# Two of the four sums of weight quadrants in each set of seven products are formed by adding transfers from DRAM instead of by VectorE

## The chip, the core and the metric

The kernel runs on one core of one Trainium2 chip, in one launch. The metric is the device time of that launch in microseconds (us); before the change the median of three runs is 1113.65 us (1112.79 to 1114.22). The core has five engines that run side by side and wait for each other on semaphores: PE (TensorE, matrix products; PEld in the profile is its loading of stationary operands), DVE (VectorE), ACT (ScalarE), POOL (GpSimd) and SP (SyncE, which here only issues transfers). Each engine takes its own instructions strictly in order, so an instruction that waits holds up everything behind it on that engine. Transfers (DMAs) are issued from the queue of an engine, here SP's or POOL's, wait there like any instruction, and run on the core's 16 DMA engines.

## The reference

A model of two layers on 512 tokens of width 1024, all in float32. Each layer mixes tokens (a gated spatial unit in the first layer, forgetting attention in the second, with attention to a memory beside both), then runs a feed-forward network of hidden width 2816. What matters here is the feed-forward network, once per layer:

```python
D_FF = -(-8 * D_MODEL // (3 * 256)) * 256
...
    h = h + rmsnorm(mixed @ w_out[layer], ln_mix_post[layer])
    f = rmsnorm(h, ln_ffn_pre[layer])
    f = (jax.nn.silu(f @ w_ffn_gate[layer]) * (f @ w_ffn_up[layer])) @ w_ffn_down[layer]
    h = h + rmsnorm(f, ln_ffn_post[layer])
```

## The kernel before

**Products in three parts.** Float32 products are made of three products in a rounded format (fp32r). Every operand is split into a high and a low part: ACT casts (`hi`, line 239), DVE subtracts (`lo`, line 240; both in `split`). `mm3` (lines 182 to 184) then issues hi·hi, hi·lo and lo·hi into one PSUM tile. Weights come from DRAM as 128 x 1024 blocks of 512 KB, called `raw`, into a ring of four buffers; `parts` turns 128 x 512 of such a block into a pair of parts, in a ring of eight pairs.

**Sets of seven products.** From the third block of 128 hidden rows on, `feed_forward` takes gate and up weights two blocks at a time. The 256 x 1024 weights of such a pair of blocks and the 1024 x 512 inputs are each cut into four quadrants, and the 2 x 2 product of quadrants is formed with seven products in place of eight, after Strassen and Winograd. That is class `Seven`: one set for gate, one for up, then the next pair of blocks. Ten pairs per layer make 20 sets, in two layers 40. Each product is 12 matmuls of 128 x 256, so a set is 84.

A set loads two blocks (line 1007): the first holds the quadrants a11 and a12 side by side, the second a21 and a22. `sums` forms four sums on DVE: s3 = a11 + a21 (line 1022, in a buffer of its own), a21 + a22 in place of a21 (line 1024), that sum + a11 in place of a11 (line 1026), and that + a12 in place of a12 (line 1027). Between them a11 and a12 are split as they came. `run` issues product by product, and splits what it needs: product 1 uses a11, 2 uses a12, 7 uses s3, 6 the new a11, 4 uses a22, 3 the new a12 and 5 the new a21. The order is 1, 7, 2, 6, 4, 3, 5. The first pair of each layer (`plain_first`) is different: both sets run 1, 2 and 3, then each runs 7 and 6, then each 4 and 5.

**PSUM.** A set has three PSUM tiles, x, a and e, of one tag, `mm` for gate and `lg` for up, with three buffers each: the third set of a layer writes the banks of the first, the fourth those of the second. A set's tiles are drained by ACT copies (lines 1040, 1049, 1052, 1055) and by `end` on DVE: e at line 1060, a at line 1061, x at line 1063. `rows` (lines 1110, 1116 and 1118) turns the results into gated hidden rows.

**Around the sets.** After three or two pairs the hidden rows go through the down weights: six or four 512 KB blocks per group, in the same ring of four raw buffers, with DVE adding the results (line 1174). Before the sets of a layer come the boundary (line 907), which norms the inputs and runs the first two hidden blocks in the ordinary way, and `combined` (line 973), in which DVE forms sums of input quadrants.

**What sets the order.** A tile framework records the program, gives each tile a buffer, places waits, and orders the instructions of each engine by its own estimate of when they can start; each engine then follows that order. So a buffer that comes free earlier may be taken by a later tile, and the order on DVE, ACT, POOL and SP is not that of the source. All weight loads are on SP's queue. POOL does little: it raises small tiles to the power −1/2 for the norms (line 253) and issues four 128 KB transfers (line 382). The s3 tile comes from a ring of four 128 x 512 buffers (`temp`, tag `t`), which a set holds until its product 7 is split.

Of the kernel before, what the change touches and what calls it, by code (L numbers as in the profile page):

```python
# [11 lines left out]
ALU = mybir.AluOpType  # L12
# [30 lines left out]
def hybrid(ctx: ExitStack, tc: tile.TileContext, i: dict, out: bass.AP):  # L43
    nc = tc.nc
# [11 lines left out]
    def name(s):  # L56
        n_of[s] = n_of.get(s, 0) + 1
        return f"{s}_{n_of[s]}"
# [7 lines left out]
    def prob(s, shape=(P, T)):  # L66
        return tp.tile(list(shape), F32, tag="p", name=name(s), bufs=6)

    def temp(s, shape=(P, T), tag="t", bufs=4, dt=F32):
        return tp.tile(list(shape), dt, tag=tag, name=name(s), bufs=bufs)  # L70
# [4 lines left out]
    def ps(tag, shape=(P, T), s="ps"):  # L75
        return pp.tile(list(shape), F32, tag=tag, name=name(s), bufs=2 if tag == "tr" else 3)

    V, A, PE, G = nc.vector, nc.scalar, nc.tensor, nc.gpsimd
# [53 lines left out]
    def loaded(src):  # L132

        raw = wp.tile([P, 1024], F32, tag="raw", name=name("raw"), bufs=4)
        last_load[0] = nc.sync.dma_start(raw, src)
        return raw
# [118 lines left out]
    class Norm:  # L255


        def __init__(self, width=T):
            self.r4 = small("r4")
            self.acc, self.width = None, width  # L260
# [25 lines left out]
        def sums(self, tb, cols):  # L286
            return [self.acc[:, c + tb * P : c + (tb + 1) * P] for c in range(0, T, self.width)]
# [711 lines left out]
    class Seven:  # L999
# [5 lines left out]
        def __init__(self, xs, src, tag, rows):  # L1005
            self.xs, self.rows = xs, rows
            w1, w2 = loaded(src(0)), loaded(src(1))
            self.a = [w[:, d : d + 512] for w in (w1, w2) for d in (0, 512)]
            self.x, self.p = ps(tag, s="x"), ps(tag, (P, 256), s="a")
            self.q = ps(tag, (P, 256), s="e")  # L1010
            self.s1, self.s2 = prob("s1"), prob("s2")
# [6 lines left out]
        def sums(self):  # L1018

            a11, a12, a21, a22 = self.a  # L1020
            self.s3 = temp("s3")
            V.tensor_add(self.s3, a11, a21)
            self.w1 = self.parts(a11)
            V.tensor_add(a21, a21, a22)
            self.w2 = self.parts(a12)
            V.tensor_add(a11, a21, a11)
            V.tensor_add(a12, a11, a12)
# [470 lines left out]
```

## Time and profile before

| What | Value |
|---|---|
| Median of three runs | 1113.65 us (1112.79 to 1114.22) |
| Span of the profiled execution | 1111.4 us |
| Mean granted TensorE clock | 0.998 |
| Instructions in the profile | 19500 |
| Read from HBM, written | 104.71 MB, 2.10 MB |
| Mean transfer rate over the span | 106 GB/s |

The profile is of one execution. Its span runs from the first to the last instruction, and the measured times hold a little around it. A row of a group gives line, engine, operation, what is written and read (out<-in), the shape and a count, then busy time, mean duration of one in ns, and the time for which the engine stood idle just before such instructions, with what ended it. A row of a timeline gives start and duration in us; instructions that follow each other are merged, with their count. `SPq` is an issue of a transfer on SP's queue. The time of a transfer to landing is counted from its issue. Tile names have lost their numbers: every weight buffer is `raw`, and `s` is both s3 and the results of a set.

### The profile page before, as it was taken

What the parts mean: (1) busy time and instruction counts of PE and PEld (TensorE: products, weight loads), DVE (VectorE), ACT (ScalarE), POOL (GpSimd) and SP (SyncE); (2) the same over time, 40 slices, a digit from 0 to 9 for tenths busy, and PEclk for the clock granted to TensorE, in tenths of its full rate; (3) what the DMA queues carried; (4) which work ended last, traced back from release to release, by engine and by line L of the source; (5) the groups of instructions that cost most, each with busy time, mean ns of one, the idle gap of its engine ahead of it and who ended that gap; (6) DMA issues with size and microseconds to landing.
All of it is one profiled execution on the core that took longest, in us unless ns stands there. A gap on an engine that the chain in (4) does not pass through costs nothing.

```text
span 1111.4 us, 19500 instructions
## 1 busy us (share of the span) xinstructions
PE 1100.8 (99%) x7382; PEld 1000.1 (90%) x7382; DVE 893.7 (80%) x1735; ACT 660.5 (59%) x1397; POOL 25.3 (2%) x42
## 2 busy tenths in 40 slices
PE   9999999999999999999999999999999999999997
PEld 7998889998899898998988898889999899899996
DVE  8889658997697597896987898858997697687875
ACT  8776468664365264577665667668665265254553
POOL 0100000000000000001000000000000000000000
PEclk9999999999999999999999999999999999999999
DMA  7522322334133323343322654422224133333222
GB/s 267 162 76 77 98 74 76 115 109 141 57 112 97 117 92 114 97 148 117 104 88 62 173 132 116 131 76 74 79 90 154 62 114 96 101 109 114 77 76 76
DMA packets 64421, 118.12 MB, mean 106 GB/s; under 512 B 5260, under 2 KB 40088, under 8 KB 64328
## 3 DMA queue, kind: packets, MB, share of 16 engines
q1 hardware_dynamic: 63720, 116.18, 33.4%
q8 instruction: 58, 0.95, 0.4%
q0 software_dynamic: 192, 0.52, 0.2%
q14 instruction: 35, 0.29, 0.1%
q10 hardware_dynamic: 416, 0.18, 0.1%
HBM read 104.71 MB, written 2.10 MB: 96 GB/s over the span
## 4 chain that ended last, share of the span: by engine, by line
PE 94%; ACT 3%; DVE 1%; issue 1%; POOL 0%; DMA 0%; POOLq 0%; DVEq 0%; ACTq 0%
PE y L182 10%; PE y L183 10%; PE y L184 10%; PE a L182 5%; PE a L184 5%; PE a L183 5%; PE x L184 3%; PE e L182 3%; PE e L184 3%; PE e L183 3%; PE x L183 3%; PE x L182 3%; PE ps L184 3%; PE ps L183 3%; PE ps L182 3%; PE v L182 2%
## 5 line engine op out<-in xcount | busy, mean ns | idle before, releaser
L239 ACT CAST whi<-raw 128x512 fp32r<-128x512 f32 x460 | 273.1, 620 | 217.7 <-PE y L184 89.1
L240 DVE TENSOR_TENSOR wlo<-raw,whi 128x512 fp32r<-128x512 f32 x460 | 303.5, 684 | 69.5 <-ACT whi L239 67.8
L182 PE MATMUL y<-whi,fhi 128*128 128x512 f32 (+1 forms) x356 | 140.2, 394 | 0.4 <-DVE y L838 0.4
L184 PE MATMUL y<-whi,flo 128*128 128x512 f32 (+1 forms) x356 | 139.3, 391 | 0.0
L183 PE MATMUL y<-wlo,fhi 128*128 128x512 f32 (+1 forms) x356 | 139.2, 391 | 0.0
L184 PE MATMUL x<-xshi,wlo 128*128 128x256 f32 x320 | 89.9, 281 | 0.0
L182 PE MATMUL a<-xshi,whi 128*128 128x256 f32 x320 | 89.8, 281 | 0.0
L183 PE MATMUL x<-xslo,whi 128*128 128x256 f32 x320 | 89.7, 280 | 0.0
L182 PE MATMUL x<-xshi,whi 128*128 128x256 f32 x320 | 89.7, 280 | 0.0
L183 PE MATMUL a<-xslo,whi 128*128 128x256 f32 x320 | 89.7, 280 | 0.0
L184 PE MATMUL a<-xshi,wlo 128*128 128x256 f32 x320 | 89.6, 280 | 0.0
L184 PEld LDWEIGHTS y<-whi,flo 128*128 128x128 f32 x356 | 66.8, 188 | 15.7
L182 PEld LDWEIGHTS y<-whi,fhi 128*128 128x128 f32 x356 | 66.8, 188 | 15.6 <-DVE y L838 0.7
L183 PEld LDWEIGHTS y<-wlo,fhi 128*128 128x128 f32 x356 | 66.9, 188 | 14.7
L182 PEld LDWEIGHTS a<-xshi,whi 128*128 128x128 f32 x320 | 60.2, 188 | 0.5
L183 PEld LDWEIGHTS a<-xslo,whi 128*128 128x128 f32 x320 | 60.2, 188 | 0.3
L184 PEld LDWEIGHTS x<-xshi,wlo 128*128 128x128 f32 x320 | 60.3, 188 | 0.0
L183 PEld LDWEIGHTS x<-xslo,whi 128*128 128x128 f32 x320 | 60.2, 188 | 0.0
L184 PEld LDWEIGHTS a<-xshi,wlo 128*128 128x128 f32 x320 | 60.2, 188 | 0.0
L182 PEld LDWEIGHTS x<-xshi,whi 128*128 128x128 f32 x320 | 60.2, 188 | 0.0
L183 PE MATMUL ps<-xslo,whi 128*128 128x256 f32 x192 | 53.9, 283 | 0.6 <-DVE xslo L240 0.6
L184 PE MATMUL ps<-xshi,wlo 128*128 128x256 f32 x192 | 54.4, 285 | 0.0
(297 smaller groups left out, 3111.1 us busy)
## 6 DMA issues: line engine op xcount, KB each, us to landing
raw<-in_w_gate SPq DMA_DIRECT2D x44, 512.0 KB, 3.5
raw<-in_w_up SPq DMA_DIRECT2D x44, 512.0 KB, 3.6
raw<-in_w_down SPq DMA_DIRECT2D x44, 512.0 KB, 3.8
raw<-in_w_out SPq DMA_DIRECT2D x16, 512.0 KB, 4.8
raw<-in_w_b_q SPq DMA_DIRECT2D x8, 512.0 KB, 3.4
raw<-in_w_a_u SPq DMA_DIRECT2D x6, 512.0 KB
raw<-in_w_v SPq DMA_DIRECT2D x6, 512.0 KB, 4.3
raw<-in_w_k SPq DMA_DIRECT2D x6, 512.0 KB
```

Source lines behind the costliest of these rows:

```text
L182: PE.matmul(o, w[0], x[0], start=start, stop=False, skip_group_check=more)
L183: PE.matmul(o, w[0], x[1], start=False, stop=False, skip_group_check=more)
L184: return PE.matmul(o, w[1], x[0], start=False, stop=stop, skip_group_check=more)
L239: last_hi[0] = A.copy(hi, src)
L240: last_split[0] = last_hi[0], (eng or V).tensor_sub(lo, src, hi)
```

## The change

```diff
--- before.py
+++ after.py
@@ -1006,6 +1006,10 @@
             self.xs, self.rows = xs, rows
             w1, w2 = loaded(src(0)), loaded(src(1))
             self.a = [w[:, d : d + 512] for w in (w1, w2) for d in (0, 512)]
+            self.s3 = temp("s3")
+            nc.sync.dma_start(self.s3, src(0)[:, :512])
+            for dst, d in ((self.s3, 0), (self.a[2], 512)):
+                G.dma_start(dst, src(1)[:, d : d + 512], accum_op=ALU.add)
             self.x, self.p = ps(tag, s="x"), ps(tag, (P, 256), s="a")
             self.q = ps(tag, (P, 256), s="e")
             self.s1, self.s2 = prob("s1"), prob("s2")
@@ -1018,10 +1022,7 @@
         def sums(self):
 
             a11, a12, a21, a22 = self.a
-            self.s3 = temp("s3")
-            V.tensor_add(self.s3, a11, a21)
             self.w1 = self.parts(a11)
-            V.tensor_add(a21, a21, a22)
             self.w2 = self.parts(a12)
             V.tensor_add(a11, a21, a11)
             V.tensor_add(a12, a11, a12)
```

For s3, SP loads a11 once more into the buffer of s3 (256 KB), and POOL issues a transfer of a21 from DRAM that adds to what the buffer holds. For a21 + a22, POOL issues a transfer of a22 from DRAM that adds to a21 where the weight load put it. The two additions on DVE are gone; those that make the new a11 and the new a12 stay. Per set that is one more issue on SP and two on POOL, and 768 KB more from DRAM.

In the order of the changed program, the a11 addition of a set is the first DVE instruction that waits for the sum a21 + a22. On POOL the adding transfer of a21 + a22 for the first set of each layer stands before the boundary's two powers (line 253), and that for the second set after them. On SP the load for s3 of set n + 4 stands before the weight loads of set n + 2. In the third set of each layer DVE has, in this order: the splits of a11 and a12 as they came, the split of s3, the a11 addition, the a12 addition, the split of the new a11, the drain of the first set's e, the splits of a22 and of the new a12, and the drains of the first set's a and x. PE's products of the third set wait for these drains: the first product for e's, the second for a's, the third for x's.

## The prediction

> **What bounds the kernel now.** I read the page first: busy time by engine, then the chain that ended last.
>
> ```profile
> PE 1100.8 (99%) x7382; PEld 1000.1 (90%) x7382; DVE 893.7 (80%) x1735; ACT 660.5 (59%) x1397; POOL 25.3 (2%) x42
> PE 94%; ACT 3%; DVE 1%; issue 1%; POOL 0%; DMA 0%; POOLq 0%; DVEq 0%; ACTq 0%
> ```
>
> PE is busy for 99% of the span, and 94% of the chain is PE. A share over the whole run can hide a stage with another limit, so next come the stretches: columns are time, then busy time of PE, PEld, DVE, ACT and POOL, granted clock, DMA share, GB/s. The first three hold sets of seven products in layer 0, the fourth in layer 1, the last is the kernel's tail.
>
> ```profile
> 203.00:242.00 39.00, 39.00 (x331) 38.94 (x330) 36.70 (x66) 24.50 (x53) 0.00 (x0) 1.00 0.34 109
> 242.00:263.00 21.00, 21.00 (x178) 20.89 (x177) 17.50 (x32) 11.62 (x27) 0.00 (x0) 1.00 0.39 121
> ...
> 296.00:356.00 60.00, 60.00 (x508) 59.87 (x507) 50.61 (x88) 34.94 (x72) 0.00 (x0) 1.00 0.32 105
> 788.00:850.00 62.00, 62.00 (x516) 61.47 (x515) 56.19 (x100) 37.37 (x80) 0.00 (x0) 1.00 0.34 111
> ```
>
> ```profile
> 1077.00:1111.00 34.00, 26.74 (x144) 22.09 (x142) 21.99 (x57) 15.41 (x34) 2.19 (x4) 0.95 0.22 62
> ```
>
> In every stretch with sets PE is busy without a break: 39.00 of 39.00, 60.00 of 60.00. DVE reaches 94% in the first (36.70 of 39.00), yet PE never waits for it there. All idle PE time of the run is 1111.4 − 1100.8 = 10.6 us, and 34.00 − 26.74 = 7.3 of it lies in the tail, which has no sets. So at most 3.3 us elsewhere could be won at all, none of it inside the sets.
>
> **What is removed.** Two additions on DVE per set, 40 sets (columns: count, busy us, mean ns of one, idle before it).
>
> ```profile
> L1024 DVE TENSOR_TENSOR raw<-raw 128x512 f32<-128x512 f32 x40 | 27.4, 684 | 0.2
> L1022 DVE TENSOR_TENSOR s<-raw,raw 128x512 f32<-128x512 f32 x40 | 27.4, 684 | 13.2 <-DMA raw<-in_w_gate 13.2
> ```
>
> That is 54.8 us of DVE work. I value it at nothing: PE's uninterrupted work in the stretches above covers it. If that cover were gone, if PE waited for DVE, it would be worth up to 54.8 us.
>
> **What is added, off the path.** (a) 40 loads of 256 KB on SP's queue. An issue takes 0.33 us (rows below), 13 us in all. They stand among the weight loads; each waits only for the split of the s3 four sets earlier, which stands before the last split of the buffer that the next weight load needs, so on SP they hold up little: the one place where that counts is in the sum. (b) 120 transfers of 256 KB, 31.5 MB more from DRAM.
>
> ```profile
> q1 hardware_dynamic: 63720, 116.18, 33.4%
> ```
>
> At 33.4% of the DMA engines for 116 MB, and counting an adding transfer twice since it must also read what it adds to, 40 × 0.26 + 80 × 0.52 = 52 MB make 15% more: under half busy on average, so nothing. (c) 80 issues on POOL. The nearest rows are four POOL transfers of 128 KB.
>
> ```profile
> L382 POOL DMA_DIRECT2D memk<-memk x4 | 2.3, 572 | 312.2 <-DVE memk L380 312.2
> ```
>
> At 0.57 us for 64 rows I take 1.1 us for 128 rows (bounds 0.57 and, twice my value, 2.3); two of them per set of 9.9 us leave POOL room. But in the changed program's order the adding transfer of the first set of each layer stands on POOL ahead of the reciprocal square root that PE's broadcast waits for.
>
> ```profile
> 172.65 0.34 SPq L135 DMA_DIRECT2D raw<-in_w_gate  x1
> ...
> 179.88 0.99 POOL L253 TENSOR_TENSOR r<-var,mhalf 128x2 f32<-128x2 f32 x1 [12.29 <-ACT sq L308]
> ```
>
> Its weights are issued at 172.65 and land 4.9 us later at most (measured below), 177.5; 1.1 us on POOL ends at 178.6, 1.3 before 179.88, and even 2.3 ends at 179.8. Nothing, then; what an issue takes beyond 2.4 us would come on top, once per layer.
>
> **What is added on the path: the wait for a21 + a22.** s3 is begun four sets ahead and cannot be late unless an adding transfer takes tens of us. The other sum can: load of the second weight tile, landing, wait on POOL, adding transfer, and only then DVE's a11 addition (L1026 before). How much time that has depends on the place. The tightest of the ordinary sets is the fifth of a layer:
>
> ```profile
> 228.80 0.33 SPq L135 DMA_DIRECT2D raw<-in_w_gate  x1
> ```
>
> ```profile
> 246.83 0.28 PE L182 MATMUL a<-d2hi,whi 128*128 128x256 f32 x1
> ```
>
> Issued at 228.80 and landed 4.9 us later, 233.7, its weights are there 13 us before PE's first product with that sum, and the addition with its split takes 2 of these. The exception is the third set of each layer, the first after the pair that runs its plain products first: its load is issued late, and in the changed order DVE has the a11 addition, with its new wait, ahead of the additions that drain the first set's PSUM tiles, whose banks the third set's first products write. Queued behind it are, in this order: the a12 addition, one split, the drain of e (frees the bank for the third set's first product), two splits, the drain of a (frees the bank for the second product). Here is that place before, on SP, DVE and PE (start us, duration us).
>
> ```profile
> 212.46 0.33 SPq L135 DMA_DIRECT2D raw<-in_w_gate  x1
> ```
>
> ```profile
> 798.66 0.33 SPq L135 DMA_DIRECT2D raw<-in_w_gate  x1
> ```
>
> ```profile
> 199.81 0.68 DVE L1022 TENSOR_TENSOR s<-raw,raw 128x512 f32<-128x512 f32 x1
> 200.41 0.68 DVE L240 TENSOR_TENSOR wlo<-raw,whi 128x512 fp32r<-128x512 f32 x1
> ...
> 217.33 0.69 DVE L1022 TENSOR_TENSOR s<-raw,raw 128x512 f32<-128x512 f32 x1 [0.42 <-DMA raw<-in_w_gate]
> ...
> 219.38 0.68 DVE L1026 TENSOR_TENSOR raw<-raw,raw 128x512 f32<-128x512 f32 x1
> 219.98 0.41 DVE L1060 TENSOR_TENSOR s<-e,s 128x256 f32<-128x256 f32 x1
> 220.32 0.68 DVE L1027 TENSOR_TENSOR raw<-raw 128x512 f32<-128x512 f32 x1
> 220.91 0.68 DVE L240 TENSOR_TENSOR wlo<-raw,whi 128x512 fp32r<-128x512 f32 x1
> 221.60 0.43 DVE L1061 TENSOR_TENSOR s<-a,s 128x256 f32<-128x256 f32 x1
> ```
>
> ```profile
> 803.61 0.69 DVE L1022 TENSOR_TENSOR s<-raw,raw 128x512 f32<-128x512 f32 x1 [0.62 <-DMA raw<-in_w_gate]
> ```
>
> ```profile
> 222.79 0.28 PE L182 MATMUL a<-xshi,whi 128*128 128x256 f32 x1
> ...
> 224.21 0.28 PE L182 MATMUL e<-t3hi,whi 128*128 128x256 f32 x1
> ```
>
> ```profile
> 808.92 0.28 PE L182 MATMUL a<-xshi,whi 128*128 128x256 f32 x1
> ...
> 810.33 0.28 PE L182 MATMUL e<-t3hi,whi 128*128 128x256 f32 x1
> ```
>
> Even before, DVE waited here for the landing (0.42 and 0.62 us), and the drains ended at 222.03, 0.8 us before PE's first product.
>
> *Landing.* From issue to the end of DVE's wait: 217.33 − 212.46 = 4.87, and 803.61 − 798.66 = 4.95. Four of the removed additions stand between 199.81 and the split that frees this buffer. DVE starts full 128x512 instructions 0.60 apart (200.41 − 199.81), so the load goes out up to 2.4 us earlier; I take 2.1, since casts on ACT sit between (bounds 0 and 2.4). The new 256 KB load goes ahead of it.
>
> ```profile
> raw<-in_w_gate SPq DMA_DIRECT2D x44, 512.0 KB, 3.5
> ...
> raw<-in_w_mem_k SPq DMA_DIRECT2D x4, 512.0 KB, 7.5
> ...
> memk<-memk POOLq DMA_DIRECT2D x4, 128.0 KB, 2.7
> ...
> out<-h SPq DMA_DIRECT2D x3, 128.0 KB, 1.9
> ```
>
> Between 128 KB in 1.9 us and 512 KB in 3.5 lie 4.2 us per MB, so 256 KB is 1.1 us; half of it overlaps, 0.6. Landing: 212.46 − 2.1 + 4.87 + 0.6 = 215.8 and 798.66 − 2.1 + 4.95 + 0.6 = 802.1.
>
> *Adding transfer.* No row shows one. Lower bound:
>
> ```profile
> DMA to landing us min/median/max: 2.4/2.7/4.8
> ```
>
> 2.4 us, the quickest POOL transfer of half the size; upper bound 7.5, the slowest group of 512 KB loads. I take 5.7: the median POOL transfer 2.7, plus 1.6 for moving 512 KB in place of 128 at 4.2 us per MB (256 KB from DRAM, as much from SBUF), plus 1.4 for the two other weight loads in flight there (4.87 against 3.5). A long tail beyond 7.5 can't be excluded, since neither row adds anything.
>
> The Trainium skill, "DMA: Bandwidth & Descriptors", section "Anatomy of one DMA — SWDGE (gpsimd) path", gives a POOL-issued transfer about 2.0 us plus its bytes at 436 GB/s, an estimate of 2.6 us for 256 KB; the sum would then be nothing. For 128 KB it gives 2.3 against the 2.7 measured here, so it is near, but it is stated for plain transfers and no trace here shows an adding one.
>
> *From there to PE.* After the sum lands at time t, DVE needs 0.60 + 0.60 + 0.75 (a cast first) + 0.35 + 0.60 + 0.60 + 0.42 = 3.9 us to the end of the second drain, and PE's second product wants it at 224.21 and 810.33: t may be 220.3 and 806.4. It is 215.8 + 5.7 = 221.5 and 802.1 + 5.7 = 807.8: late by 1.2 and 1.4 us. PE then runs behind for good, since it has no idle time to catch up in.
>
> **Sum.** Against the profiled execution, 1111.4 + 2.6 = 1114.0. The measured median, 1113.65, is 2.3 us above that span, which no edit touches, so the forecast is **1116.3 us**. The unit of measurement that can be told from no change is 0.2%, 2.2 us; the forecast is only just past it.
>
> **Rivals.**
> *Hidden.* The sum lands within 4.4 us; PE never notices: 1113.7. For it: the 2.7 us POOL transfers and the skill's rule. Against: the transfers in flight at just that place. This ends on the other side, not slower. It decides at 220.3 − 215.8 = 4.5 and 806.4 − 802.1 = 4.3 us.
> *Slow addition.* An adding transfer takes 10 us: 5.5 us at each of the two places, 1124.7, with about 1 us more per layer at the fifth set. Above some 9.6 us the ring of four weight buffers turns into the bound. Two sets take PE 2 × 7 × 1.42 = 19.9 us (12 matmuls from 222.79 to 224.21); load 4.9, transfer, and seven splits and two additions at 0.60, 5.4, have to fit. At 15 us it would cost 2.7 us on each of some 36 sets, about 1210 us. For it: no row shows an adding transfer. Against: POOL rows at 2.4 to 4.8.
> *Relief reaches PE.* DVE's freed 54.8 us shorten the 3.3 us that PE loses outside the tail: if two thirds or more went, 1111.4. Against: those gaps lie outside the sets, with other instructions waited for.
>
> **Chances.** Forecast (4.4 to 9 us per adding transfer, 1113.7 to 1123) 0.48, of which 0.33 past the bound; hidden 0.26; slow 0.21; relief 0.05. Slower by over 0.2%: 0.33 + 0.21 = 0.54. Within: 0.15 + 0.24 + 0.01 = 0.40. Faster: 0.02 + 0.04 = 0.06. Range 1112.5 to 1128: it takes in the hidden case with a us of scatter and the slow one up to about 11 us; what it leaves out is a far slower transfer and half of the relief. The forecast's own range is 1113.7 to 1123.
>
> **What would show it.** Landing of the adding transfers: 4.5 to 7 us, longest where four loads are in flight. POOL: some 1.1 us per issue. DVE busy down by about 55 us, PE busy the same. Around 222 and 809 us PE idle 1 to 1.5 us before the third set's first two products, released by the drains on DVE, and DVE idle ahead of the a11 addition, ended by a POOL transfer. No such PE gap: hidden. PE gaps before later sets too, or a11 additions waiting in most sets: slow addition. A gap before the broadcast near 181 and 767 us would say that POOL's queue was the price. A shorter time with PE's idle unchanged would break the whole argument, since then the pace of the matmuls themselves would have moved.

## The result and the profile after

The changed kernel takes 1122.99 us (median of 4 runs, 1122.20 to 1124.84) against 1113.56 us (4 runs, 1112.79 to 1114.22): ratio 1.0088, 95% interval 1.0073 to 1.0102. It is slower by 9.4 us; the forecast's sum was 2.6. The profiled execution has a span of 1120.7 us, 9.3 above that of before.

The page of the changed kernel: busy time, then two DMA queues (packets, MB, share of 16 engines), then the chain that ended last.

```profile
PE 1104.6 (99%) x7382; PEld 1003.8 (90%) x7382; DVE 850.9 (76%) x1655; ACT 662.1 (59%) x1397; POOL 94.0 (8%) x122
...
q1 hardware_dynamic: 69480, 126.67, 36.8%
q0 software_dynamic: 11712, 21.50, 12.0%
...
PE 90%; DVE 3%; ACT 3%; DMA 2%; issue 1%; POOL 0%; POOLq 0%; DVEq 0%; ACTq 0%
```

DVE has 42.8 us less to do, and yet PE is later. The number to look at is PE's: busy time went from 1100.8 to 1104.6 (3.8 us more, with the same 7382 matmuls), and idle time from 10.6 to 1120.7 − 1104.6 = 16.1 (5.5 more). Both together are the 9.3 us. Busy time that grows with the same matmuls means that some of them ran slower.

The four stretches that the prediction shows for the kernel before, now of the changed kernel (time; busy time of PE, PEld, DVE, ACT and POOL; granted clock, DMA share, GB/s):

```profile
203.00:242.00 39.00, 35.44 (x287) 35.23 (x286) 29.15 (x50) 22.46 (x48) 6.76 (x8) 0.96 0.80 200
242.00:263.00 21.00, 21.00 (x180) 20.96 (x179) 18.20 (x32) 12.95 (x28) 2.56 (x3) 1.00 0.71 187
296.00:356.00 60.00, 60.00 (x489) 59.01 (x488) 48.56 (x82) 35.04 (x71) 7.67 (x9) 1.00 0.65 167
788.00:850.00 62.00, 59.19 (x464) 57.77 (x464) 50.31 (x89) 37.65 (x79) 11.50 (x14) 0.97 0.75 183
```

PE still works without a break in two of the four; it lost time only where the first sets of a layer lie. There the DMA share rose from 0.34 to 0.80 and 0.75, and the clock, 1.00 before, is 0.96 and 0.97. In the other two the DMA share rose as well, to 0.71 and 0.65, and PE lost nothing.

PE's waits in the changed kernel (engine, line, what it waited for; us in total, times, longest):

```profile
PE a L182 <- DVE s L1061: 6.4, 2, 3.6
PE yt L871 <- DVE yg L858: 2.3, 1, 2.3
```

One new entry, two waits of 6.4 us together, both for the drain of e on DVE (line 1061, 1060 before). Its timelines in layer 0, on POOL, DVE and PE, and POOL and DVE in layer 1:

```profile
216.43 0.86 POOL L1012 DMA_DIRECT2D raw<-in_w_gate  x1 [2.54 <-DVE wlo L240]
```

```profile
223.90 0.69 DVE L1027 TENSOR_TENSOR raw<-raw,raw 128x512 f32<-128x512 f32 x1 [6.90 <-DMA raw<-in_w_gate]
224.63 0.69 DVE L1028 TENSOR_TENSOR raw<-raw 128x512 f32<-128x512 f32 x1
225.34 0.69 DVE L240 TENSOR_TENSOR wlo<-raw,whi 128x512 fp32r<-128x512 f32 x1
225.94 0.42 DVE L1061 TENSOR_TENSOR s<-e,s 128x256 f32<-128x256 f32 x1
```

```profile
226.42 0.38 PE L182 MATMUL a<-xshi,whi 128*128 128x256 f32 x1 [3.56 <-DVE s L1061]
...
237.95 0.28 PE L182 MATMUL a<-xshi,whi 128*128 128x256 f32 x1
```

```profile
807.40 0.86 POOL L1012 DMA_DIRECT2D raw<-in_w_gate  x1 [3.53 <-DMA raw<-in_w_gate]
```

```profile
814.09 0.69 DVE L1027 TENSOR_TENSOR raw<-raw,raw 128x512 f32<-128x512 f32 x1 [5.83 <-DMA raw<-in_w_gate]
```

PE's stop in layer 1:

```profile
816.60 0.39 PE L182 MATMUL a<-xshi,whi 128*128 128x256 f32 x1 [2.81 <-DVE s L1061]
```

This is the chain of the forecast, link by link: POOL issues the adding transfer of the third set at 216.43; DVE stands at the a11 addition for 6.90 us until it lands; the a12 addition and a split go first, and only then comes the drain that PE's first product needs. From POOL's issue to DVE's restart it is 7.47 us here and 6.69 in layer 1.

The second part of the loss is behind the stop. The third set's first matmul is at 226.42 and the fourth set's at 237.95, 11.53 us later. Before, the fourth set's first matmul is this one, 232.68 − 222.79 = 9.89 us after the third's:

```profile
232.68 0.28 PE L182 MATMUL a<-xshi,whi 128*128 128x256 f32 x1
```

PE does not wait once in those 11.53 us. The granted clock says why (stretches of the changed kernel, columns as above):

```profile
223.88:227.29 3.41, 0.87 (x7) 0.88 (x8) 3.34 (x6) 2.61 (x6) 1.43 (x2) 1.00 0.95 131
227.29:230.70 3.41, 3.41 (x18) 3.41 (x18) 3.41 (x8) 2.18 (x6) 0.00 (x0) 0.50 0.92 202
814.39:817.80 3.41, 1.20 (x10) 1.20 (x11) 3.36 (x7) 2.93 (x7) 1.37 (x2) 1.00 0.89 127
817.80:821.21 3.41, 3.41 (x19) 3.41 (x18) 3.41 (x8) 2.18 (x6) 0.00 (x0) 0.50 0.95 235
```

For 3.41 us behind each stop the clock is 0.50, and 18 or 19 matmuls run where 29 did (3.41 / 0.118). That is 11.53 − 9.89 = 1.64 us per stop. Two stops of 6.4 us together and two stretches at half clock, 3.3 us, are 9.7; 0.4 of it was won back elsewhere. This says where the time lies in this trace. Whether the 3.3 us would be saved without the half clock is another question, and an experiment below bears on it.

### The profile page after: what moved, and what is told of

Read it like the earlier page. It is cut to its first block, busy times and chain, and to the rows that moved or that the text cites. A ratio compares the mean times of both kernels' runs of the same rounds, so it can differ in the third digit from the quotient of the medians.

```text
span 1120.7 us, 19829 instructions
## 1 busy us (share of the span) xinstructions
PE 1104.6 (99%) x7382; PEld 1003.8 (90%) x7382; DVE 850.9 (76%) x1655; ACT 662.1 (59%) x1397; POOL 94.0 (8%) x122
## 3 DMA queue, kind: packets, MB, share of 16 engines
q1 hardware_dynamic: 69480, 126.67, 36.8%
q0 software_dynamic: 11712, 21.50, 12.0%
## 4 chain that ended last, share of the span: by engine, by line
PE 90%; DVE 3%; ACT 3%; DMA 2%; issue 1%; POOL 0%; POOLq 0%; DVEq 0%; ACTq 0%
PE y L182 9%; PE y L183 9%; PE y L184 9%; PE a L182 5%; PE a L183 5%; PE a L184 5%; PE ps L184 3%; PE x L182 3%; PE x L183 3%; PE x L184 3%; PE ps L183 3%; PE e L182 3%; PE e L183 3%; PE e L184 3%; PE ps L182 3%; DMA raw<-in_w_gate 2%
```

## The experiments

All edits are to the changed kernel unless said otherwise. Times of before in the same sessions were 1113.5 to 1113.9 us. A bracket is the 95% interval of the ratio to before.

**Third set on DVE again.**

```diff
-            for dst, d in ((self.s3, 0), (self.a[2], 512)):
+            for dst, d in ((self.s3, 0), (self.a[2], 512))[: 1 if third else 2]:
...
+            if self.third:
+                V.tensor_add(a21, a21, a22)
```

> Only the third set of each layer forms a21 + a22 on DVE again; 118 of the 120 new transfers stay. Lateness theory (all that is lost is lost at those two sets): no PE gap near 222 and 809 us, no stretch at half clock behind them, 1113.5 us within 1. Rival, traffic (31 MB more from DRAM and 80 issues on POOL slow the kernel as such): the time stays near 1122.99, at least above 1120.

1114.22 us, 1.0004 [0.9995, 1.0012]. Both stops and both stretches at half clock are gone, with 118 of the 120 transfers still there. Two transfers out of 120 carry the loss; traffic and issues as such do not. One stop of 1.1 us is new, in layer 1, for a copy on ACT (line 1055); such copies come up again below.

**No sums at all.**

```diff
-            self.s3 = temp("s3")
-            nc.sync.dma_start(self.s3, src(0)[:, :512])
-            for dst, d in ((self.s3, 0), (self.a[2], 512)):
-                G.dma_start(dst, src(1)[:, d : d + 512], accum_op=ALU.add)
...
-                self.product(self.q, self.parts(self.s3), 1)
+                self.product(self.q, self.parts(self.a[3]), 1)
```

> The two sums are left out altogether, additions and transfers both: a21 is used where a21 + a22 belongs, and a22 where s3 belongs. This is DVE's relief with no price. Prediction's theory (PE covers that DVE work): 1113.5 us within 1. Rival, relief reaches PE: 1111.4 or less.

1113.44 us, 0.9997 [0.9989, 1.0006]. DVE is as free as in the changed kernel (850.4 us busy) and nothing is paid for it, and the time is that of before. DVE's relief is worth nothing that can be measured. The interval also bounds what any version of this idea can be expected to win from that relief: 0.1%.

**What makes the transfer long.** Two kernels at the same place: one in which the POOL transfers overwrite instead of adding, one without those of s3.

```diff
-                G.dma_start(dst, src(1)[:, d : d + 512], accum_op=ALU.add)
+                G.dma_start(dst, src(1)[:, d : d + 512])
```

> The 80 POOL transfers stay, with their places, sizes and waits, but they overwrite instead of adding: both sums are left out. If the adding itself (reading the target, too) makes the transfer long: the median landing falls from 5.3 us to about 2.7 + 0.5 = 3.2 (the 128 KB POOL transfer, plus 128 KB at 4.2 us per MB), in the third set from 7.4 to about 4.5, the sum's place is filled at about 221 us, and PE's gap there shrinks to 1 us or less: 1114 to 1116 us. Rival, the queue and the loads beside it make it long: landing stays at 5 us or more, at the third set at 7, and the time at 1122.

1121.03 us, 1.0064 [1.0051, 1.0078]. POOL issue and DVE's restart in the third set of layer 0:

```profile
216.88 0.54 POOL L1012 DMA_DIRECT2D raw<-in_w_gate  x1 [3.76 <-DMA raw<-in_w_gate]
```

```profile
222.78 0.69 DVE L1027 TENSOR_TENSOR raw<-raw,raw 128x512 f32<-128x512 f32 x1 [5.25 <-DMA raw<-in_w_gate]
```

From the page, the queue of the POOL transfers (11712 packets and 12.0% with the addition), and from the view of the line the landing of all 80 with and without the addition, the latter first:

```profile
q0 software_dynamic: 6592, 21.50, 5.9%
```

```profile
DMA to landing us min/median/max: 2.8/3.5/7.2
```

```profile
DMA to landing us min/median/max: 4.0/5.3/8.9
```

The addition makes the median landing 1.8 us longer, and at the place that counts 7.47 − (222.78 − 216.88) = 1.57 us. For the same 21.50 MB the packets of this queue take twice the time (12.0% of the 16 engines' span against 5.9%; 0.2% and 192 packets of both belong to four other transfers). So the addition is part of the delay, but the transfer that only overwrites still takes 5.90 us there, and PE still stops for 1.91 us. The first theory was near with the median (3.2 expected, 3.5 measured) and wrong about this place. PE's stop in layer 1 is 0.9 us, and one more, of 0.8, is for a copy on ACT; with half clock behind the first stop that is some 5.2 of the 7.3 us by which this kernel is slower than before. The rest was not traced to a place.

```diff
-            self.s3 = temp("s3")
-            nc.sync.dma_start(self.s3, src(0)[:, :512])
-            for dst, d in ((self.s3, 0), (self.a[2], 512)):
+            for dst, d in ((self.a[2], 512),):
...
-                self.product(self.q, self.parts(self.s3), 1)
+                self.product(self.q, self.parts(self.a[3]), 1)
```

> The new loads of s3 and its adding transfers are left out (a22 is used where s3 belongs); the 40 adding transfers of a21 + a22 stay. If the s3 transfers in flight beside it (213.05 to 220.55 us in the changed kernel) stretch the adding transfer of the third set: it takes 5 us instead of 7.4, the sum lands near 221.4 and PE waits 1 to 1.5 us there without a stretch at half clock: about 1116. Rival, an adding transfer takes 7 us at that place by itself: gap of 3 us and half clock as in the changed kernel, 1121 or more.

1117.49 us, 1.0031 [1.0019, 1.0043]. POOL, DVE and PE at the third set, and the landing of all 40:

```profile
215.67 0.84 POOL L1010 DMA_DIRECT2D raw<-in_w_gate  x1 [21.41 <-DMA raw<-in_w_up]
```

```profile
221.59 0.69 DVE L1025 TENSOR_TENSOR raw<-raw,raw 128x512 f32<-128x512 f32 x1 [4.65 <-DMA raw<-in_w_gate]
```

```profile
224.10 0.39 PE L182 MATMUL a<-xshi,whi 128*128 128x256 f32 x1 [1.30 <-DVE s L1059]
```

```profile
DMA to landing us min/median/max: 3.9/4.1/5.8
```

Still adding, but without s3's transfers beside it, the transfer takes 221.59 − 215.67 = 5.92 us there, 1.55 less than in the changed kernel. PE's stop shrinks to 1.30 us (0.8 in layer 1), as expected, with no half clock behind it. The time is 1.5 us above what was expected; PE has two further stops of 0.8 us, one in the fourth set of each layer, for copies on ACT.

**Only s3 by transfers.**

```diff
-            for dst, d in ((self.s3, 0), (self.a[2], 512)):
+            for dst, d in ((self.s3, 0),):
...
+            V.tensor_add(a21, a21, a22)
```

> Only s3 is formed by transfers (an SP load and an adding transfer per set); a21 + a22 is on DVE again in all sets. The sum that PE waited for is then there without a transfer. Lateness theory: no gap at the third sets, 1113.5 us within 1. Rival, s3's transfers delay the weight loads of the third set (the load goes out behind s3's on SP): a gap of 1 us or more at 222 us, 1116.

1116.57 us, 1.0025 [1.0014, 1.0036]. Both theories failed. The stop at the third set is 0.2 us, yet 2.8 us are lost. PE's waits, then ACT and DVE at the second of the new stops:

```profile
PE e L182 <- ACT s L1057: 1.6, 2, 0.8
...
PE a L182 <- DVE s L1062: 0.2, 1, 0.2
```

```profile
238.93 1.29 ACT L1113 ACTIVATE s<-s 128x512 f32<-128x512 f32 x2 [1.24 <-DVE s L1112]
240.13 0.35 ACT L1057 COPY s<-e 128x256 f32<-128x256 f32 x1
```

```profile
237.62 0.68 DVE L1065 TENSOR_TENSOR s<-x,s 128x512 f32<-128x512 f32 x1
238.21 1.28 DVE L1112 TENSOR_TENSOR s<-s,rbc 128x512 f32<-128x512 f32 x2
```

PE's product 4 of the fourth set waits for the copy of e on ACT (line 1057). In ACT's order the two Silu of the gate set stand ahead of it, and they wait for DVE (line 1112). The order that the framework planned around the transfers has no slack here. In the changed kernel the same order cost PE nothing, since the stop ahead of it had already made PE late.

**DVE's order alone, all transfers kept.**

```diff
-            V.tensor_add(a11, a21, a11)
+            with behind(*([drains[-1]] if self.third else ())):
+                V.tensor_add(a11, a21, a11)
...
-                self.product(self.x[:, right], self.parts(a12), 5)
+                w = self.parts(a12)
+                if self.third:
+                    with behind(last_split[0][1]):
+                        pending.pop()()
+                self.product(self.x[:, right], w, 5)
...
-        for u in us:
-            u.end()
+        us[0].end()
+        pending.append(us[1].end)
```

> All 120 transfers stay. In the third set DVE drains the first set's e, a and x before the a11 addition, and drains the second set only after the splits that the third set needs. Lateness theory: the sum comes as late as in the changed kernel (about 223.9 us), but only drains queued behind it made PE wait; product 6, the first that uses the sum, is needed by PE at 222.8 + 3 x 1.42 = 227.1, and 223.9 + 0.6 + 0.75 + 0.6 = 225.9 is in time. No gap, 1113.5 us within 1. Rival, the sum itself is too late for the products: a gap of 1 us or more moves to product 6, 1116 or more. Rival, traffic: 1122.99 as before.

1116.65 us, 1.0027 [1.0018, 1.0036]. In the third set the a11 addition now stands behind the drains of the first set, and the drains of the second set behind the splits that the third set needs. The sum comes as late as ever (DVE's a11 addition at 223.99), and PE has no stop at 222 or 809 us. What had stopped it was the drain behind the wait. Of 9.4 us 6.3 come back. The rest is again that copy on ACT, now at the sixth set of each layer:

```profile
PE e L182 <- ACT s L1061: 2.6, 2, 1.3
```

**ACT's order, on top of it, and by itself.**

```diff
-            A.activation(g, g, AF.Silu, scale=-1.0 if row else 1.0)
             gates[row] = g
+            silu = lambda: A.activation(g, g, AF.Silu, scale=-1.0 if row else 1.0)
+            silu() if m == 2 else silus.append(silu)
...
-                A.copy(s2[:, right], self.q)
+                with behind(A.copy(s2[:, right], self.q)):
+                    while silus:
+                        silus.pop(0)()
```

> All 120 transfers stay, DVE's order of e2_drains_first stays. On ACT the two Silu of a gate set come behind the copy of e in the following up set (they wait for DVE, and in e2_drains_first PE waited for that copy: 1.46 us in each layer, and 0.39 and 0.47 beside). Theory (what is left is order on ACT, not the transfers): the 1.46 us gaps go, 1113.7 to 1115 us. Rival, the adding transfers of the sixth set (6.5 us there) are late by themselves: gaps of 1 us or more stay, 1116.5.

> e7_only_s3 with the Silu behind the copy of e, as above; nothing else moves on any engine. In e7_only_s3 PE waited 0.93 and 0.96 us at the fourth set of each layer for that copy. Theory (ACT's order): these two go, 1116.57 - 1.9 = 1114.7 us. Rival (s3's transfers or the POOL issues cost it): 1116.5.

> The changed kernel with only ACT's order altered as in e10_silu_behind_copy (Silu behind the copy of e); DVE's order stays, the drains stand behind the a11 addition. Lateness theory: the two stops of 3.7 and 3.0 us with their half clock stay, for they come from DVE's order: 1122 to 1123.5 us. Rival, ACT's order alone was the loss, and the drains did not matter: 1114 to 1116.

| ACT's order | DVE's order as changed | drains ahead of the a11 addition | only s3 by transfers |
|---|---|---|---|
| as planned | 1122.99, 1.0088 [1.0073, 1.0102] | 1116.65, 1.0027 [1.0018, 1.0036] | 1116.57, 1.0025 [1.0014, 1.0036] |
| Silu behind the copy of e | 1124.73, 1.0102 [1.0085, 1.0118] | 1113.81, 1.0001 [0.9992, 1.0010] | 1114.26, 1.0004 [0.9995, 1.0013] |

With both orders mended, all 120 transfers cost nothing that can be measured. The DVE timeline of that kernel still shows the wait, with the sum as late as ever, and its list of PE waits has neither the drain of e (line 1068 here) nor a copy on ACT:

```profile
224.13 0.69 DVE L1028 TENSOR_TENSOR raw<-raw,raw 128x512 f32<-128x512 f32 x1 [1.48 <-DMA raw<-in_w_gate]
```

In layer 1 PE works without a break, beside a DMA share of 0.79 (columns as above):

```profile
788.00:850.00 62.00, 62.00 (x518) 61.47 (x517) 49.76 (x89) 37.75 (x80) 10.34 (x13) 1.00 0.79 196
```

ACT's order by itself wins nothing for the changed kernel (1124.73, 1.2 us above what was expected): the two stops, 6.2 us together, come from DVE's order and stay. None of these versions beats the kernel before, as the run without sums had already bounded.

**The half clock.** Matmuls whose result nothing reads are put on PE ahead of the third set's first product.

```diff
             if what == 1:
+                if self.third:
+                    with behind(last_mm[0]):
+                        o = ps("tr", s="fill")
+                        for _ in range(24):
+                            PE.matmul(o[:, :256], self.xs[0][0][0][:, :P], self.xs[0][0][0], start=True, stop=True)
                 self.product(self.p, self.w1, 0)
```

> The changed kernel, with 24 matmuls whose result nothing reads (24 x 0.118 = 2.8 us) on PE ahead of the third set's first product, inside the gap; 0.9 and 0.1 us of PE idle remain. If the idle PE itself brings the 3.41 us at half clock: no such stretch, the third set takes 10.05 us again in place of 11.7, and the time is 1122.99 - 2 x 1.65 = 1119.7 us within 0.7. Rival, the third set is slow because its own operands come late, whatever PE did before: 11.7 us again, 1123.

1126.28 us, 1.0113 [1.0100, 1.0126]: slower still, and neither expectation came true. The planner moved two casts on ACT ahead of the copy of the third set's first product, and PE stopped for 2.6 us in each layer at product 6 instead. That run is inconclusive on the cost, but it has stretches worth reading. The first two follow each other in layer 0, the last two in layer 1:

```profile
229.11:232.53 3.42, 1.79 (x16) 1.58 (x14) 3.42 (x7) 2.22 (x4) 0.00 (x0) 1.00 0.46 140
232.53:235.94 3.41, 2.42 (x20) 2.42 (x21) 3.41 (x7) 1.95 (x6) 0.00 (x0) 1.00 0.49 159
...
823.04:826.45 3.41, 1.51 (x12) 1.51 (x13) 3.41 (x7) 2.64 (x6) 0.00 (x0) 1.00 0.38 92
826.45:829.86 3.41, 3.41 (x18) 3.41 (x17) 3.41 (x8) 2.03 (x4) 0.86 (x1) 0.50 0.43 141
```

Two stops of 2.6 us, one with half clock behind it and one without. In layer 0 the stop is spread over two stretches, of which the fuller has PE idle for 3.42 − 1.79 = 1.63 us; in layer 1 one stretch holds 1.90.

> The 24 matmuls in the gap again. In the run e4_filled ACT's copy of the third set's first product came behind two casts and PE lost 2.8 us there in place of the half clock; here these casts are put behind that copy and the copy of product 7, as in the changed kernel. If PE's idle time brings the half clock: no stretch at half clock behind 226 us, product 6 starts 1.65 us earlier than in the changed kernel, at 230.7 in place of 232.4, and if nothing else is late then, the time is 1119.7. Rival, the operands of the later products would have been late anyway and the half clock hid it: a new gap of 1 to 2 us at product 6, 4 or 3, and 1121 to 1123.

Here the two casts are held behind the copies. 1122.94 us, 1.0082 [1.0069, 1.0096]. There is no half clock behind 226 or 817 us, so PE's idle time is what brings it. But the time is that of the changed kernel, as the rival expected: PE now stops at later products for copies on ACT (0.35, 0.28 and 0.53 us in layer 0, start to start beyond the usual pitch, and as much in layer 1). So part of what the slow clock takes in the changed kernel, by these figures 1.16 of 1.64 us, would have been lost to late operands anyway. What the half clock costs by itself, these two runs cannot say.

> The changed kernel with 12 matmuls in the gap in place of 24: PE idles for some 2.3 us in layer 0 and some 1.5 in layer 1. So far idle stretches of 2.07 us and more brought half clock (one of 2.78 did not), and none of 1.47 or less. If the length of the idle stretch decides: half clock after 226 us, none after 817. If any idle stretch at this place brings it: both. If only 2.5 us and more: neither.

1123.12 us (one run). The stops came out at 2.8 us in layer 0, 1.0 at 816 us and 1.5 at 822 us, since the order on ACT moved here too. Half clock stands behind the first alone, which has PE idle for 3.41 − 1.56 = 1.85 us in one stretch:

```profile
225.24:228.65 3.41, 1.56 (x13) 1.51 (x13) 3.36 (x8) 3.24 (x7) 0.84 (x1) 1.00 0.86 125
228.65:232.07 3.42, 3.42 (x17) 3.42 (x17) 3.42 (x7) 1.26 (x2) 0.00 (x0) 0.50 0.63 172
815.74:819.16 3.42, 2.45 (x19) 2.18 (x19) 3.40 (x8) 2.93 (x7) 0.04 (x1) 1.00 0.93 138
```

So not every idle stretch at this place brings half clock. Nor does it need a stop of 2.5 us: the kernel whose transfers only overwrite has it behind one of 1.91.

## Why the forecast held, and which term was too small

- *Relief on DVE is worth nothing.* Shown: 0.9997 without the sums and without transfers. DVE's busy time fell by 42.8 us, not 55. Busy time counts an overlap once, and in a row of full instructions one of 0.68 us starts every 0.60, so 80 additions hold some 48 us; the remaining 5 are not accounted for.
- *Loads on SP, more traffic, issues on POOL cost nothing.* Shown by the kernel with all 120 transfers and mended order, 1.0001. An issue takes 0.86 to 0.89 us in the mean, not 1.1. The issue ahead of the boundary's power did no harm: PE's wait for the broadcast is 0.5 us in two places, as before. "Under half busy on average" was true of the run (36.8% and 12.0%) and said nothing of the stage that decided, where the share was 0.80.
- *The place.* The third set of each layer, the drains queued behind the a11 addition, nothing else in the ordinary sets: all as forecast, and shown by putting the sum of those two sets back on DVE. The forecast let the drain of a decide, 0.2 us tighter than that of e; the trace has e's.
- *Landing of the weights.* Forecast 215.8; POOL issued the adding transfer at 216.43, and at 807.40 in layer 1, where 802.1 was forecast and PE was by then 5 us late. In the trace's semaphore records the weights had landed at 215.91 (where the row names a split on DVE as what ended POOL's wait) and 806.84; POOL's issue follows about half a microsecond later both times, a step that the sum did not have.
- *The adding transfer: the term that was mis-sized.* Taken at 5.7 us, it was 7.47 and 6.69. Its parts, against the forecast's: without s3's transfers the median of all adding transfers lands in 4.1 us (2.7 + 1.6 = 4.3 in the forecast). At the third set it takes 5.92, so what else is in flight there, the weight loads, costs some 1.8 (1.4 in the forecast). The remaining 1.55 us go with the loads and adding transfers of s3, which the change itself puts there and which the forecast did not count as company. With 7.47 in place of 5.7 the forecast's own sum gives 1.2 + 1.8 = 3.0 us late in layer 0, and with the landing 0.6 later 3.6: PE's wait was 3.56.
- *"PE then runs behind for good."* True, but PE lost more than its waits. In the trace of the changed kernel the rest is the 3.41 us at half clock, 1.64 us behind each stop, about a third of the loss. With PE kept busy in the stop there is no half clock, other operands come late instead, and the time is the same. So what the forecast lacked is that a stop has a sequel, in the clock or in the order behind it; it priced a stop at its length. Of its own signs, "PE busy the same" did not hold: PE was busy for 3.8 us more.
- *The size.* 1122.99 us lies in the forecast's own range, 1113.7 to 1123, at its very end, and 9.4 us is three and a half times the sum. That range was drawn for transfers of up to 9 us. With the 7.47 and 6.69 that were measured the forecast's arithmetic gives 3.0 + 2.4 = 5.4 us, some 1119; with the stops as they were, 6.4, it is 1120. Place, wait and direction were foreseen; that the range reached the measured time was in part luck.
- *The rivals.* Hidden would have needed 4.4 us; without s3's transfers an adding transfer takes less in the median, 4.1, but not at this place. Slow addition gives nearly the time that was measured (1124.7) by another way: 10 us per transfer did not happen at these places, and no ring of buffers became the bound.
- *The Trainium skill's figure.* The transfers that only overwrite land in 2.8 us at best and 3.5 in the median, 0.2 and 0.9 above the estimate of 2.6 from "DMA: Bandwidth & Descriptors", section "Anatomy of one DMA — SWDGE (gpsimd) path". For plain transfers the trace agrees with it at best, and the median is a third longer; it was rightly not carried over to adding ones, of which the section says nothing, at 4.0 to 8.9.

## What to carry to other kernels

An instruction that gets a new wait must be priced with what stands behind it on its engine: here the data came in time for the products that use it, and a drain that did not need it was what stopped PE. Work moved from an idle-enough engine to a transfer gains nothing where PE is the bound, and can leave an order without slack; look for the one place in the stage with the least lead, and count as traffic there what the change itself adds. When one stop is removed, look for the stop that it had covered.

## What the runs showed of the hardware

**A stop that fills a little over half of a 3.41 us window is followed by half clock.** By the trace's record of the granted clock, the changed kernel's stretches at half clock start at 227.29, 817.80 and 1114.76 us: 173.0 and 87.0 times 3.413 us apart. Cut into stretches on that grid, the traces of all kernels here show half clock in the stretch behind one at full clock with PE idle for 1.85 us or more (the least were 1.85, 1.90 and 1.91, the most 2.91), and none behind one at full clock with 1.72 or less. The line lies between these two, a little over half of 3.41. (The first microseconds of a run are left out. A stretch that is itself at half clock is another case: in the changed kernel's tail one with PE idle for 1.45 us was followed by more half clock.) What the half clock costs by itself is not shown. A stop of 2.6 us was followed by half clock or not according to where it fell on the grid. The Trainium skill, "TensorE: Matmul & The Clock Gate", section "What's actually happening", describes a free-running window of 3413 ns, and the grid agrees. The same page, section "Why this matters for your kernels", warns of idle gaps of more than about 3 us; here 1.91 us, within one window, was enough:

```profile
223.06:226.47 3.41, 1.50 (x13) 1.29 (x12) 3.36 (x7) 2.91 (x7) 0.54 (x1) 1.00 0.37 129
226.47:229.88 3.41, 3.41 (x19) 3.41 (x18) 3.41 (x8) 2.17 (x6) 0.00 (x0) 0.50 0.41 154
```

These two stretches are from the kernel whose transfers only overwrite.

**Adding on the way costs the transfer.** For 256 KB from DRAM into SBUF: 3.5 us in the median without and 5.3 with the addition, 78% more packets on the queue (11712 against 6592), twice the time of its packets, and 0.84 to 0.86 us in place of 0.54 in the median for the issue on POOL.
